# Delta heads: value projected first and turned by VectorE and permuting loads, instead of by TensorE chunk by chunk

## The chip, the cores and the metric

The kernel runs on one core of one Trainium2 chip. The metric is the device time of one execution in microseconds (us); the figure for a kernel is the median of its runs. A core has TensorE (PE: matmuls, and PEld: loads of the stationary operand), VectorE (DVE), ScalarE (ACT), GpSimd (POOL) and SyncE (SP), each with its own queue of instructions in order; SP, ACT and POOL issue the DMAs here.

## The reference

A hybrid residual block on 1024 tokens of width 1024: a gated linear attention branch of 4 heads, a gated delta branch of 8 heads of width 128, a gated merge of both, then an MLP with squared ReLU. What matters here is one delta head:

```python
d_qkv = jax.nn.silu(causal_short_conv(d_qkv, gdn_conv_w))     # 4 taps
q, k = l2_norm(q), l2_norm(k)
# per chunk, with the triangular solve giving u and w
v_new = uu - w @ state
o     = (q * exp(gc)) @ state + att @ v_new
state = dec * state + k_state.T @ v_new
...
o_d = rms_norm(o_d, gdn_onorm_w) * silu(d_g)
```

## The kernel before, in words

All products are in float32 split into a high and a low part, three passes each. Every projection of the delta branch is one call of `dense_b`: 8 steps (`dense_k`) of 6 matmuls 128x512, into one of two PSUM tiles `pm` with channels on the partitions and 1024 tokens along the row. A delta head is `gdn_head(h)`, which calls `dense_b` three times: 24 steps. After each step `tick()` advances a clock, and `on(t, fn)` puts work of the head into an agenda that runs it t steps after the head's begin. So the order on each engine is the order of this agenda, between the steps of the dense product; a number above 24 means that the work runs under the next head's projections. The names in the trace: `pm<-hH,wH`, `pm<-hL,wH`, `pm<-hH,wL` are the three passes of a dense step; `cv` is a projection after its convolution, `si` its tanh, and a product of the two makes silu; `pa` is any of four small PSUM banks.

The projections come in the order q, value, gate. `conv_silu` takes the three taps, the tanh and the silu of one; q's run at ticks 9 to 14, the value's at 18 to 22. `att` (two halves) makes q times k per chunk on TensorE at ticks 15 and 16, VectorE multiplies by the decays `Dt`. `squares` (`qj`) and `qd` (q times the decay, in `eg`) are at 15. `ktok` (`kt`), k with tokens on the partitions, comes from DRAM through four permuting loads of POOL, each of 32 partitions in pieces of 32 floats.

The state goes through 8 chunks of 128 tokens, each in three ticks. `c0(t)`, tick 24 + 3t: TensorE turns the value's chunk (a matmul with `ident`) into a fresh bank and adds `ke` times the state `st` to it, ScalarE scales it to `rs`. `c1(t)`, a tick later: the inverse `U` times `rs`, which ScalarE copies twice, scaled (`vs`) and plain (`vn`; both are halves of one tile, named `vn` in the trace). `c2(t)`: `kt` times `vs` gives the state's update, which VectorE adds (`st`), and two products give the output in `po`. The outputs of heads 0 to 4 then go through a norm whose factors are laid out by two DMAs (`on_d`, `row`). `u1`, `u2`, `u3` complete the head's inverse at ticks 7, 10 and 13. During head 7 the merging stage starts, with branch weights `wB` (POOL and SP) and stored outputs `xq` (SP).

The weights of projections come in the order of a table, `plan`, whose last entry tells which engine makes the low part.

Of the kernel before, what the change touches and what calls it, by code (L numbers as in the profile page):

```python
# [8 lines left out]
F32 = mybir.dt.float32  # L9
# [3 lines left out]
AF = mybir.ActivationFunctionType  # L13
ALU = mybir.AluOpType
# [5 lines left out]
NT = 8  # L20
EPS = 1e-6
C_AQ, C_AK, C_AV, C_AG, C_LR = 0, 512, 1024, 2048, 3072
C_DQ, C_DK, C_DV, C_DG, C_BETA, C_DA, C_MA, C_MD = 3088, 4112, 5136, 6160, 7184, 7192, 7200, 8224
# [27 lines left out]
def block_kernel(ctx: ExitStack, tc: tile.TileContext, x, c, ada_w, ada_b, pre_mix_w, post_mix_w,  # L51
# [3 lines left out]
    x, ada_w, w_in, gla_w_lr = x[0], ada_w[0], w_in[0], gla_w_lr[0]  # L55
# [4 lines left out]
    sm = ctx.enter_context(tc.tile_pool(name="sm", bufs=3))  # L60
# [4 lines left out]
    dr = ctx.enter_context(tc.tile_pool(name="dr", bufs=1, space=DRAM))  # L65

    V, A, G, T = engines = [InOrder(tc, e) for e in (nc.vector, nc.scalar, nc.gpsimd, nc.tensor)]
# [3 lines left out]
    def nm(p):  # L71
        uid[0] += 1
        return f"{p}{uid[0]}"
# [3 lines left out]
    def t4(shape=(128, 1024), dt=F32, p="t", tag="w4"):  # L77
        return w4.tile(list(shape), dt, tag=tag, name=nm(p), bufs=tag_bufs[tag])
# [4 lines left out]
    def pat(shape=(128, 512)):  # L83
        return pa.tile(list(shape), F32, tag="pa", name=nm("pa"))
# [58 lines left out]
    vt = t4((95, 128), p="vt")  # L143
# [277 lines left out]
    for hh in range(4):  # L421
        plan += [(w_in, C_AQ + hh * 128, 128, 8, V), (w_in, C_AK + hh * 128, 128, 8, V),
                 (w_in, C_AV + hh * 256, 256, 4, V), (w_in, C_AG + hh * 256, 256, 8, V)]
    plan += [(w_in, c0 + h * 128, 128, 8, E) for h in range(8) for c0, E in ((C_DQ, (1, 5) if h else (4, 6)), (C_DV, (1, 3)), (C_DG, (1, 4)))]

    def conv_w_later(raw_ap, shape, dh, dl, src=None):

# [18 lines left out]
    def splits():  # L446
        early = {}

        def load(e):
            early[e] = load_raw(*plan[e][:3])  # L450

        first = next(e for e, p_ in enumerate(plan) if p_[1] == C_DQ)
        for e, (w, c0, n, kt, E) in enumerate(plan):
            raw = early.pop(e) if e > first else load_raw(w, c0, n)
            if e < 3:
                for i in range(2):
                    part = raw[:, :, i * 128:(i + 1) * 128]
                    yield conv_w_later(part, (128, 8, 128), *E) if e or i else conv_w_tile(part, (128, 8, 128), E=V)
            elif type(E) is tuple:
                if e + 1 < len(plan):  # L460
                    at(E[1] + 1, lambda: load(e + 1))
                yield conv_w_later(raw, (128, 8, 128), *E)
            elif kt == 4:
                yield [conv_w_tile(raw[:, 4 * i:4 * i + 4, :], (128, 4, 256), E=E) for i in range(2)]
            else:
                for i in range(n // 128):
                    yield conv_w_tile(raw[:, :, i * 128:(i + 1) * 128], (128, 8, 128), E=E)
        yield None
# [8 lines left out]
    def dense_b(rhs):  # L477
        wH, wL = next_w()
        ps = pmt()
        for k in range(8):  # L480
            dense_k(ps, wH, wL, rhs, k)
            tick()
        return ps
# [425 lines left out]
    oa_d = [dr.tile([2, 128, 1024], F32, name=f"oa_d{i}") for i in range(4)]  # L909
    od_d = [dr.tile([2, 128, 1024], F32, name=f"od_d{i}") for i in range(4)]  # L910
    on_d = [dr.tile([1024], F32, name=f"on_d{h}") for h in range(8)]
    kg_d = [dr.tile([128, 1024], F32, name=f"kg_d{h}") for h in range(4)]

    def gdn_head(h, then=None):
# [3 lines left out]
        def on(t, fn):  # L918
            at(begin + t - clock[0], fn)
# [38 lines left out]
        def conv_silu(ps, ct, t, late=0):  # L958

            y, u = t4(p="cv"), {}  # L960
            A.activation(y, ps, AF.Copy, scale=ccol[:, 3 * 24 + ct:3 * 24 + ct + 1])

            def tap(s_):
                V.scalar_tensor_tensor(y[:, s_:], ps[:, :S - s_], ccol[:, (3 - s_) * 24 + ct:(3 - s_) * 24 + ct + 1],
                                       y[:, s_:], ALU.mult, ALU.add)

            def tanh():
                u["t"] = t4(p="si")
                A.activation(u["t"], y, AF.Tanh)

            t += late
            for s_ in (1, 2, 3):
                on(t + s_, lambda s_=s_: tap(s_))
            on(t + 4, tanh)
            on(t + 6 - late, lambda: V.scalar_tensor_tensor(y, u["t"], 1.0, y, ALU.add, ALU.mult))
            return y

        on(7, u1)
        on(10, u2)
        on(13, u3)  # L980
        psq = dense_b(h_rhs)

        q = conv_silu(psq, h, 8)
        z, turned = {}, h < 5
        vq = None if turned else small(8, "vq")

        def att(hf):
            if not hf:
                z["att"] = t4(p="attT")
            pt = pat()  # L990
            for i in range(4):
                sl = slice((hf * 4 + i) * 128, (hf * 4 + i + 1) * 128)
                T.matmul(pt[:, i * 128:(i + 1) * 128], kT[:, sl], q[:, sl], start=True, stop=True)
            on(16 + hf, lambda: V.tensor_mul(z["att"][:, hf * 512:(hf + 1) * 512], pt, Dt[:, hf * 512:(hf + 1) * 512]))

        def squares():
            z["qj"] = t4(p="qj")
# [29 lines left out]
        qd = eg  # L1027
        on(13, lambda: A.activation(eg, eg, AF.Exp))
        on(13, lambda: V.tensor_tensor(ke, kT, ke, ALU.mult))
        on(15, lambda: att(0))  # L1030
        on(16, lambda: att(1))
        on(15, squares)
        on(15, lambda: V.tensor_tensor(qd, q, eg, ALU.mult))
        on(28, lambda: token_part(0))
        on(30, lambda: token_part(1))
        if not turned:
            on(32, token_total)
        psv = dense_b(h_rhs)

        vv = conv_silu(psv, 16 + h, 16, 1)  # L1040
        so = small(32, "so", 1) if turned else small(8, "so", 2)
        c = {"st": None}

        def c0(t):

            sl = slice(t * 128, (t + 1) * 128)
            pv = c["pv"] = pat()
            T.matmul(pv[:, 0:128], vv[:, sl], ident, start=True, stop=(t == 0), is_transpose=True)
            if t:
                T.matmul(pv[:, 0:128], ke[:, sl], c["st"], start=False, stop=True)  # L1050
            rs = c["rs"] = sm.tile([128, 128], F32, tag="rs", name=nm("rs"), bufs=2)
            A.activation(rs, pv[:, 0:128], AF.Copy, scale=rbC[:, h * 8 + t:h * 8 + t + 1])

        def c1(t):

            pv = c["pv"][:, 128:256]
            T.matmul(pv, U[:, t, :], c["rs"], start=True, stop=True)
            v2 = c["vn"] = sm.tile([128, 256], F32, tag="gst", name=nm("vn"), bufs=3)
            if t < NT - 1:
                A.activation(v2[:, 0:128], pv, AF.Copy, scale=ksC[:, h * 8 + t:h * 8 + t + 1])  # L1060
            A.copy(v2[:, 128:256], pv)

        def c2(t):
            sl = slice(t * 128, (t + 1) * 128)
            i, hf, st, vs, vn = t % 4, t // 4, c["st"], c["vn"][:, 0:128], c["vn"][:, 128:256]
            if t < NT - 1:
                pS = c["pv"][:, 256:384]
                T.matmul(pS, ktok[:, sl], vs, start=True, stop=True)
                sn = c["st"] = sm.tile([128, 128], F32, tag="st", name=nm("st"), bufs=3)
                if t:  # L1070
                    V.scalar_tensor_tensor(sn, st, decB[:, h * 8 + t:h * 8 + t + 1], pS, ALU.mult, ALU.add)
                else:
                    A.copy(sn, pS)
            if i == 0:
                c["po"] = pat()
            po = c["po"]
            for j, (l, r) in enumerate(((vn, z["att"][:, sl]), (st, qd[:, sl]))[:1 + min(t, 1)]):
                l, r = (l, r) if turned else (r, l)
                T.matmul(po[:, i * 128:(i + 1) * 128], l, r, start=j == 0, stop=j == min(t, 1))
            if i == 3:  # L1080
                on(47 + late if hf else 35, lambda: (outs if turned else results)(hf, po))
# [42 lines left out]
        def sums(hf):  # L1124
            if not hf:
                c["t"] = t4(p="sqt")
            h_ = slice(hf * 512, (hf + 1) * 512)
            V.transpose(c["t"][:, h_], c["sq"][:, h_])
            V.reduce_sum(so[:, hf * 16:(hf + 1) * 16], r3(c["t"][:, h_], 16), axis=mybir.AxisListType.X)
# [22 lines left out]

        def times():
            V.tensor_mul(sg, sg, c["row"])
            on(75, lambda: A.dma_start(od_d[h // 2][h % 2], sg))
            dump("odT", sg, lambda t: t[h * 128:(h + 1) * 128, :])

        def last_on(t, fn):
# [7 lines left out]
            then()  # L1166
        if turned:
            for t, fn in ((48, lambda: half_squares(0)), (50, lambda: half_squares(1)), (53, lambda: sums(0)),
                          (56, lambda: sums(1)), (58, gated), (59, groups), (62, roots), (66, rows), (72, times)):
                last_on(t, fn)  # L1170
        else:
            on(48 + end, norm)
            on(50 + end, scale)
            on(52 + f_, lambda: fin(0))
            on(53 + f_, lambda: fin(1))
# [1382 lines left out]
```

## Time and profile before

| | |
|---|---|
| median of 3 runs | 1872.37 us (1872.29 to 1873.21) |
| profiled execution | 1873.31 us, its span 1871.6 us |
| TensorE busy | 1845.7 us, 99% |
| VectorE busy | 1415.8 us, 76% |
| ScalarE busy | 864.2 us, 46% |
| GpSimd busy | 204.4 us, 11% |
| mean granted clock of TensorE | 0.998 |
| DMA | 318.00 MB, mean 170 GB/s |

The delta heads run from about 560 to 960 us of the span. All work is recorded with the line of one helper, line 38, so groups are told apart by their tiles. A row of a timeline gives start, duration, engine, operation, output from inputs, and in brackets how long the engine sat idle before it and for whom; PEld idle before a load is not always idle time of PE.

### The profile page before, as it was taken

Reading aid. Unit: us, or ns where it says so; the run is one execution under the profiler, and the core shown is the slowest. Engines: PE = TensorE matmul, PEld = TensorE weight load, DVE = VectorE, ACT = ScalarE, POOL = GpSimd, SP = SyncE. Lnnn points to the kernel's source line nnn. Section 1 sums busy time; section 2 is a strip of 40 time slices with the busy share of each in tenths; the row PEclk is TensorE's granted clock in tenths of the full one; section 3 lists DMA queues with packets and bytes.
Section 4 is the critical chain, followed back from the end, with each engine's and each line's share of the span. In section 5 each row is a group of like instructions: output and inputs, shape, how many; then the busy total and the mean of one; then the engine's idle time right before and its main releaser. Section 6 shows DMA issues by size and latency. Waiting matters only on the chain. (4 is left out here: it accounts for less than half of the span.)

```text
span 1871.6 us, 26161 instructions
## 1 busy us (share of the span) xinstructions
PE 1845.7 (99%) x10025; PEld 1547.4 (83%) x10025; DVE 1415.8 (76%) x2205; ACT 864.2 (46%) x1389; POOL 204.4 (11%) x196
## 2 busy tenths in 40 slices
PE   7999999999999999999999999999999999999998
PEld 5788888989888888888888888878888888888886
DVE  5785844968766677778788688986687877778887
ACT  5454324243333444444654555568545446343333
POOL 2120111111120011111101001000022210000001
PEclk9999999999999999999999999999999999999999
DMA  9686573324235454555868757346667668163425
GB/s 317 219 259 192 154 170 102 107 74 136 68 103 173 112 145 134 157 146 174 242 180 205 231 142 195 90 172 210 206 220 252 210 236 308 57 226 112 157 102 102
DMA packets 255070, 318.00 MB, mean 170 GB/s; under 512 B 73474, under 2 KB 179408, under 8 KB 254944
## 3 DMA queue, kind: packets, MB, share of 16 engines
q1 hardware_dynamic: 222032, 272.63, 45.3%
q0 software_dynamic: 16640, 28.73, 7.9%
q10 hardware_dynamic: 16272, 14.95, 2.5%
q8 instruction: 79, 1.29, 0.3%
q14 instruction: 47, 0.39, 0.1%
HBM read 233.77 MB, written 82.51 MB: 169 GB/s over the span
## 5 line engine op out<-in xcount | busy, mean ns | idle before, releaser
L38 PE MATMUL pm<-hH,wH 128*128 128x512 f32 x864 | 284.7, 410 | 0.0
L38 PE MATMUL pm<-hL,wH 128*128 128x512 f32 x864 | 269.3, 392 | 0.0
L38 PE MATMUL pm<-hH,wL 128*128 128x512 f32 x864 | 267.5, 390 | 0.0
L38 PE MATMUL pm<-oH,wB 128*128 128x512 f32 x672 | 214.8, 394 | 0.6 <-DMA wB<-in_w_branch_gla_dram 0.6
L38 PE MATMUL pa<-w,yH 128*128 128x512 f32 (+1 forms) x696 | 212.5, 387 | 0.0
L38 PEld LDWEIGHTS pm<-hH,wL 128*128 128x128 f32 x864 | 161.7, 188 | 35.5
L38 PEld LDWEIGHTS pm<-hL,wH 128*128 128x128 f32 x864 | 161.9, 188 | 34.9
L38 PEld LDWEIGHTS pm<-hH,wH 128*128 128x128 f32 x864 | 147.1, 190 | 19.2 <-issue 0.2
L38 DVE TENSOR_TENSOR w<-raw,w 128x512 fp32r<-128x512 f32 (+1 forms) x144 | 125.8, 876 | 40.9 <-ACT w L38 40.0
L38 PEld LDWEIGHTS pa<-w,yH 128*128 128x128 f32 x696 | 130.1, 188 | 27.0 <-DVE ya L38 0.4
L38 PEld LDWEIGHTS pm<-oH,wB 128*128 128x128 f32 x672 | 126.1, 188 | 26.8 <-DMA wB<-in_w_branch_gla_dram 1.1
L38 ACT CAST w<-raw 128x512 fp32r<-128x512 f32 (+1 forms) x144 | 99.5, 711 | 89.3 <-DVE raw L38 80.0
L38 PE MATMUL pa<-w,yL 128*128 128x512 f32 (+1 forms) x348 | 134.5, 387 | 0.0
L38 PE MATMUL pm<-oL,wB 128*128 128x512 f32 x336 | 130.8, 389 | 0.0
L38 ACT CAST wH<-raw 128x1024 fp32r<-128x1024 f32 x62 | 64.4, 1046 | 112.8 <-PE pm L38 72.1
L38 PE MATMUL pa<-oB,w 128*128 128x512 f32 x480 | 111.9, 391 | 0.8 <-DVE oB L38 0.5
L38 PEld LDWEIGHTS pa<-oB,w 128*128 128x128 f32 x480 | 89.6, 188 | 20.2 <-DVE oB L38 1.2
L38 DVE TENSOR_TENSOR wL<-raw,wH 128x1024 fp32r<-128x1024 f32 x62 | 75.4, 1219 | 38.2 <-ACT wH L38 37.6
L38 DVE SCALAR_TENSOR_TENSOR cv<-pm,ccol,cv 128x1023 f32<-128x1023 f32 (+2 forms) x72 | 91.9, 1276 | 8.5 <-ACT cv L38 7.4
L38 PE MATMUL pa<-oT,w 128*128 128x512 f32 x384 | 90.8, 389 | 0.0
L38 PE MATMUL pm<-oT,w 128*128 128x512 f32 x384 | 90.8, 389 | 0.0
L38 DVE TENSOR_TENSOR ya<-pa,ya 128x512 f32<-128x512 f32 (+1 forms) x83 | 56.0, 682 | 43.7 <-PE pa L38 43.7
(427 smaller groups left out, 3750.0 us busy)
## 6 DMA issues: line engine op xcount, KB each, us to landing
yL<-y_d SPq DMA_DIRECT2D x53, 512.0 KB, 7.4
raw<-in_mlp_w_dram SPq DMA_DIRECT2D x23, 1024.0 KB, 6.1
raw<-in_w_in_dram SPq DMA_DIRECT2D x18, 1024.0 KB, 7.3
raw<-in_w_in_dram SPq DMA_DIRECT2D x32, 512.0 KB, 4.9
araw<-in_ada_w_dram SPq DMA_DIRECT2D x32, 512.0 KB, 3.8
raw<-in_mlp_w_dram SPq DMA_DIRECT2D x18, 512.0 KB, 4.9
araw<-in_ada_w_dram SPq DMA_DIRECT2D x32, 256.0 KB, 6.6
sl<-sg_d SPq DMA_DIRECT2D x16, 512.0 KB, 7.3
```

The costliest lines, as they stand in the source:

```text
L38: r = fn(*args, **kw)
```

## The change

Delta heads project value, q, gate. The value's conv and silu come first (silu now a tick earlier, at 13). `v_turn` transposes it in 32x32 blocks on VectorE (two instructions of 128x512, tick 14), SP stores it to a new DRAM tile `v_d` (tick 15), and POOL loads it back in four pieces that permute the blocks, as `kt` does, into `vt` with tokens on the partitions (tick 17). `att`, `squares` and `qd` move from ticks 15 and 16 to 23 and 24. In the chunks, `c0` has no transpose: for the first chunk `rs` is made from `vt` in SBUF; for later ones the state product is accumulated on the value that `c1` of the chunk before has copied (ScalarE, `vt` to PSUM) over the place from which `vs` and `vn` were read. The `kt` product in that bank no longer starts its group anew. The last product of the norm and its store move by one tick.

On TensorE, the first and second ticks of a chunk (second chunk of head 1), before:

```order
L38 MATMUL pm_6018<-hH_562,wL_5971 128x512 x2
L38 MATMUL pa_6050<-ident,cv_5905 128x128
L38 MATMUL pa_6050<-st_6038,ke_5760 128x128
L38 MATMUL pm_6018<-hH_564,wH_5921 128x512 x2
L38 MATMUL pm_6018<-hL_579,wH_5921 128x512 x2
L38 MATMUL pm_6018<-hH_564,wL_5971 128x512 x2
L38 MATMUL pa_6050<-rs_6053,U_5337 128x128
```

and after, in the same place:

```order
L38 MATMUL pm_6040<-hH_570,wL_5980 128x512 x2
L38 MATMUL pa_6047<-st_6063,ke_5777 128x128
L38 MATMUL pm_6040<-hH_572,wH_5931 128x512 x2
L38 MATMUL pm_6040<-hL_587,wH_5931 128x512 x2
L38 MATMUL pm_6040<-hH_572,wL_5980 128x512 x2
L38 MATMUL pa_6093<-rs_6075,U_5345 128x128
```

The product with `ident` is gone; the state product goes into the bank of the chunk before, and the product with `U` takes a new one.

On ScalarE, in the same chunk of head 1, before:

```order
L38 ACTIVATE rs_6053<-pa_6050,rbC 128x128
L38 ACTIVATE vn_6071<-pa_6050,ksC 128x128
L38 COPY vn_6071<-pa_6050 128x128
L38 ACTIVATE rs_6102<-pa_6099,rbC 128x128
L38 ACTIVATE vn_6111<-pa_6099,ksC 128x128
```

and after:

```order
L38 ACTIVATE rs_6075<-pa_6047,rbC 128x128
L38 ACTIVATE vn_6095<-pa_6093,ksC 128x128
L38 COPY vn_6095<-pa_6093 128x128
L38 COPY pa_6093<-vt_5926 128x128
L38 ACTIVATE rs_6124<-pa_6093,rbC 128x128
L38 ACTIVATE vn_6135<-pa_6133,ksC 128x128
```

A copy from `vt` follows `vn`, into the bank from which the next `rs` is made and into which the product with `kt` goes next; that product waits for ScalarE, now for this copy.

On POOL, at the loads of head 2, before:

```order
L38 DMA on_d_485<-sqt_6088 32x32
L38 DMA kt_6537<-kt_d_451 32x32x32
L38 DMA row_6335<-on_d_485 128x1024
L38 DMA kt_6537<-kt_d_451 32x32x32 x3
L38 DMA on_d_486<-sqt_6492 32x32
```

and after:

```order
L38 DMA on_d_485<-sqt_6113 32x32
L38 DMA vt_6334<-v_d_495 32x32x32 x4
L38 DMA row_6351<-on_d_485 128x1024
L38 DMA kt_6570<-kt_d_451 32x32x32 x4
L38 DMA on_d_486<-sqt_6525 32x32
```

The four loads of `vt` stand between the store of the norm's factors and the load of their row; the next head's `kt` follows. In head 7 the loads of `vt` stand behind one load of branch weights `wB`.

The diff, without the table's line (it exchanges q and value in `plan` and keeps the engines by place) and the two lines of `times` (72 to 73, 75 to 76):

```diff
+    v_d = [dr.tile([128, 1024], F32, name=f"v_d{h}") for h in range(8)]
...
-            on(t + 6 - late, lambda: V.scalar_tensor_tensor(y, u["t"], 1.0, y, ALU.add, ALU.mult))
+            on(t + 5 - late, lambda: V.scalar_tensor_tensor(y, u["t"], 1.0, y, ALU.add, ALU.mult))
...
-        psq = dense_b(h_rhs)
-
-        q = conv_silu(psq, h, 8)
+        psv = dense_b(h_rhs)
+        vv = conv_silu(psv, 16 + h, 8)
...
-            on(16 + hf, lambda: V.tensor_mul(z["att"][:, hf * 512:(hf + 1) * 512], pt, Dt[:, hf * 512:(hf + 1) * 512]))
+            on(24 + hf, lambda: V.tensor_mul(z["att"][:, hf * 512:(hf + 1) * 512], pt, Dt[:, hf * 512:(hf + 1) * 512]))
...
-        on(15, lambda: att(0))
-        on(16, lambda: att(1))
-        on(15, squares)
-        on(15, lambda: V.tensor_tensor(qd, q, eg, ALU.mult))
+
+        def v_turn():
+            z["vb"] = t4(p="vb")
+            for h_ in (slice(0, 512), slice(512, 1024)):
+                V.transpose(z["vb"][:, h_], vv[:, h_])
+
+        def v_load():
+            z["vt"] = t4(p="vt")
+            src = v_d[h].rearrange("(c i) (t b j) -> b i t c j", i=32, t=8, j=32)
+            for b_ in range(4):
+                G.dma_start(z["vt"][32 * b_:32 * b_ + 32].rearrange("i (t c j) -> i t c j", t=8, j=32), src[b_])
+
+        on(14, v_turn)
+        on(15, lambda: DMA.dma_start(v_d[h], z["vb"]))
+        on(17, v_load)
+        on(23, lambda: att(0))
+        on(24, lambda: att(1))
+        on(23, squares)
+        on(23, lambda: V.tensor_tensor(qd, q, eg, ALU.mult))
...
-        psv = dense_b(h_rhs)
-
-        vv = conv_silu(psv, 16 + h, 16, 1)
+        psq = dense_b(h_rhs)
+        q = conv_silu(psq, h, 16, 1)
...
-            pv = c["pv"] = pat()
-            T.matmul(pv[:, 0:128], vv[:, sl], ident, start=True, stop=(t == 0), is_transpose=True)
+            rs = c["rs"] = sm.tile([128, 128], F32, tag="rs", name=nm("rs"), bufs=2)
+            src = z["vt"][:, sl]
             if t:
-                T.matmul(pv[:, 0:128], ke[:, sl], c["st"], start=False, stop=True)
-            rs = c["rs"] = sm.tile([128, 128], F32, tag="rs", name=nm("rs"), bufs=2)
-            A.activation(rs, pv[:, 0:128], AF.Copy, scale=rbC[:, h * 8 + t:h * 8 + t + 1])
+                src = c["pv"][:, 128:256]
+                T.matmul(src, ke[:, sl], c["st"], start=False, stop=True, skip_group_check=True)
+            A.activation(rs, src, AF.Copy, scale=rbC[:, h * 8 + t:h * 8 + t + 1])
...
-            pv = c["pv"][:, 128:256]
+            bank = c["pv"] = pat()
+            pv = bank[:, 128:256]
...
             A.copy(v2[:, 128:256], pv)
+            if t < NT - 1:
+                A.copy(pv, z["vt"][:, (t + 1) * 128:(t + 2) * 128])
...
-                T.matmul(pS, ktok[:, sl], vs, start=True, stop=True)
+                T.matmul(pS, ktok[:, sl], vs, start=False, stop=True, skip_group_check=True)
```

More of the change, by code (lines that the diff above doesn't have):

```diff
@@ L423, in block_kernel @@
                  (w_in, C_AV + hh * 256, 256, 4, V), (w_in, C_AG + hh * 256, 256, 8, V)]
-    plan += [(w_in, c0 + h * 128, 128, 8, E) for h in range(8) for c0, E in ((C_DQ, (1, 5) if h else (4, 6)), (C_DV, (1, 3)), (C_DG, (1, 4)))]
+    plan += [(w_in, c0 + h * 128, 128, 8, E) for h in range(8) for c0, E in ((C_DV, (1, 5) if h else (4, 6)), (C_DQ, (1, 3)), (C_DG, (1, 4)))]
     def conv_w_later(raw_ap, shape, dh, dl, src=None):
@@ L450, in load @@
             early[e] = load_raw(*plan[e][:3])
-        first = next(e for e, p_ in enumerate(plan) if p_[1] == C_DQ)
+        first = next(e for e, p_ in enumerate(plan) if p_[1] == C_DV)
         for e, (w, c0, n, kt, E) in enumerate(plan):
@@ L1154, in times @@
             V.tensor_mul(sg, sg, c["row"])
-            on(75, lambda: A.dma_start(od_d[h // 2][h % 2], sg))
+            on(76, lambda: A.dma_start(od_d[h // 2][h % 2], sg))
             dump("odT", sg, lambda t: t[h * 128:(h + 1) * 128, :])
@@ L1168, in gdn_head @@
             for t, fn in ((48, lambda: half_squares(0)), (50, lambda: half_squares(1)), (53, lambda: sums(0)),
-                          (56, lambda: sums(1)), (58, gated), (59, groups), (62, roots), (66, rows), (72, times)):
+                          (56, lambda: sums(1)), (58, gated), (59, groups), (62, roots), (66, rows), (73, times)):
                 last_on(t, fn)
```

## The prediction

> **What bounds the kernel now.** I read the busy shares first, then the windows of the delta stage, then who waits for whom there.
>
> ```profile
> span 1871.6 us, 26161 instructions
> PE 1845.7 (99%) x10025; PEld 1547.4 (83%) x10025; DVE 1415.8 (76%) x2205; ACT 864.2 (46%) x1389; POOL 204.4 (11%) x196
> ```
>
> The windows' first and last of that stage (PE, PEld, DVE, ACT, POOL busy, then clock, DMA share, GB/s):
>
> ```profile
> 585.00:635.00 50.00, 50.00 (x293) 42.22 (x292) 30.86 (x41) 17.62 (x35) 4.64 (x6) 1.00 0.39 114
> 885.00:935.00 50.00, 49.45 (x296) 41.58 (x295) 36.94 (x47) 32.18 (x68) 7.77 (x6) 1.00 0.88 254
> ```
>
> TensorE is busy for 50.00 of 50 us early and 49.45 late, at clock 1.00. Time is won by taking work off TensorE and lost by making it wait; work elsewhere is free until TensorE waits for it. The waits from 570 to 1000 us (total us, times, longest):
>
> ```profile
> ACT rs L38 <- PE pa L38: 107.6, 60, 5.6
> ...
> ACT si L38 <- PE pa L38: 9.4, 5, 1.9
> ...
> PEld pa L38 <- ACT vn L38: 2.9, 8, 0.5
> ...
> PEld pa L38 <- DVE st L38: 1.4, 2, 0.9
> ```
>
> ScalarE waits for TensorE all the time; the other way, the weight queue waits for `vn` only 8 times and for the state twice.
>
> **Transposes removed.** One per chunk and head:
>
> ```profile
> L38 PE MATMUL pa<-ident,cv x64: 270/272/274, 593.8 to 958.2; 128*128 128x128 f32 x64
> ```
>
> By durations that is 64 x 0.272 = 17.4 us. But durations of a pipelined engine overlap, so I take distances between starts, each over four matmuls of the dense product and whatever stands between them:
>
> ```profile
> 567.78 0.62 PE L38 MATMUL pm<-hH,wL 128*128 128x512 f32 x2
> ...
> 568.68 0.39 PE L38 MATMUL pm<-hL,wH 128*128 128x512 f32 x1
> ...
> 593.30 0.62 PE L38 MATMUL pm<-hH,wL 128*128 128x512 f32 x2
> ...
> 594.33 0.63 PE L38 MATMUL pm<-hL,wH 128*128 128x512 f32 x2
> 594.79 0.62 PE L38 MATMUL pm<-hH,wL 128*128 128x512 f32 x2
> ...
> 595.93 0.63 PE L38 MATMUL pm<-hL,wH 128*128 128x512 f32 x2
> ...
> 598.23 0.62 PE L38 MATMUL pm<-hH,wL 128*128 128x512 f32 x2
> 598.69 0.27 PE L38 MATMUL pa<-ident,cv 128*128 128x128 f32 x1
> ...
> 599.48 0.39 PE L38 MATMUL pm<-hL,wH 128*128 128x512 f32 x1
> ```
>
> With nothing between, 0.90; with a transpose alone (the first chunk of a head, 593.30), 1.03; with the one product of the next step (594.79), 1.14; with transpose and state product (598.23), 1.25. So a transpose costs 0.13 alone and 1.25 - 1.14 = 0.11 beside a product. Saved: 8 x 0.13 + 56 x 0.11 = **7.2 us**; 17.4 would be the upper end.
>
> The Trainium skill ("TensorE: Matmul & The Clock Gate", Part 4: PE-mode transpose) gives about 275 ns for a 128x128 transpose inside a kernel. The row's 272 ns agrees as a duration; were it the cost of the slot, the sum would gain 17.6 us. The four distances speak against that.
>
> **The copy added.** After `vs` and `vn` of a chunk ScalarE copies the next chunk's value into PSUM, 7 x 8 = 56 times; by the order below, the product with `kt` now waits for it. No copy from SBUF to PSUM is in this trace. Nearest: copies and what uses them.
>
> ```profile
> 595.93 0.26 ACT L38 COPY vn<-pa 128x128 f32<-128x128 f32 x1
> 596.08 1.06 ACT L38 CAST wH<-raw 128x1024 fp32r<-128x1024 f32 x1
> ...
> 684.58 0.59 ACT L38 COPY ob<-pa 128x512 f32<-128x512 f32 x1 [1.57 <-PE pa L38]
> ...
> 686.40 0.62 ACT L38 ACTIVATE sqo<-ob 128x512 f32<-128x512 f32 x1
> ```
>
> ```profile
> 596.63 0.42 PEld L38 LDWEIGHTS pa<-vn,kt 128*128 128x128 f32 x2
> ```
>
> A 128x128 copy takes 0.26; a source in SBUF (sqo, 0.62) costs 0.03 more than one in PSUM (ob, 0.59). At best the copy starts 0.15 after `vn` does, as the cast at 596.08, and ends 0.15 after `vn`'s end at 596.19. But it overwrites what `vn` reads, so I take the other end: it starts when `vn` ends and takes 0.30, to 596.49. The weight load stands at 596.63 without having waited. The copy therefore fits with 0.14 to spare, and costs nothing in an ordinary step; the cover is gone once it takes over about 0.4. As ScalarE's time, 56 x 0.30 = 17 us lie in an engine busy 17.6 to 32.2 of 50.
>
> It costs where the load already waits for `vn`:
>
> ```profile
> 664.34 1.06 ACT L38 ACTIVATE si<-cv 128x1024 f32<-128x1024 f32 x1 [1.87 <-PE pa L38]
> ...
> 665.55 0.25 ACT L38 COPY vn<-pa 128x128 f32<-128x128 f32 x1
> ```
>
> ```profile
> 665.86 0.30 PEld L38 LDWEIGHTS pa<-vn,kt 128*128 128x128 f32 x2 [0.49 <-ACT vn L38]
> ...
> 911.57 0.30 PEld L38 LDWEIGHTS pa<-vn,kt 128*128 128x128 f32 x2 [0.20 <-ACT vn L38]
> ...
> 921.90 0.31 PEld L38 LDWEIGHTS pa<-vn,kt 128*128 128x128 f32 x2 [0.15 <-ACT vn L38]
> ```
>
> At 665.86 the tanh held ScalarE (itself waiting for TensorE, 5 such waits in all, in five heads), and the load began 0.06 after `vn` ended. Each of the 8 waits grows by the copy: 8 x 0.30 = **+2.4 us** (1.2 if it overlaps `vn`). Behind the waiting load stand the output products and the next dense step, so this is TensorE's own time.
>
> **Moved work.** The attention products, `qj` and `qd` go from ticks 15 and 16 to 23 and 24: the same count, so nothing for TensorE as long as q is ready; its silu ends near tick 22, and one tick (two passes of 0.90 hold four of six matmuls) is over 1.35 us. In head 7, tick 23 meets the merging stage:
>
> ```profile
> 929.69 0.34 DVE L38 SCALAR_TENSOR_TENSOR st<-st,decB,pa 128x128 f32<-128x128 f32 x1
> ```
>
> ```profile
> 930.09 0.30 PEld L38 LDWEIGHTS pa<-st,ke 128*128 128x128 f32 x2 [0.91 <-DVE st L38]
> ```
>
> There the load already waits 0.91 for the state. The moved `qd` (about 1.21, the size of the row at 666.82 below) and two attention halves now come just ahead on VectorE, and `qj` ahead of `vn` on ScalarE. Between 0 and their 2.6 us, I take **+1.2**, the one full-size multiply.
>
> **The value's new way.** v is turned on VectorE, stored by SP (512 KB), loaded by POOL in four permuting pieces. VectorE's 16 halves of 0.70 are 11 us of an engine that is busy 31 to 37 of 50.
>
> ```profile
> 666.82 1.21 DVE L38 SCALAR_TENSOR_TENSOR cv<-si,cv 128x1024 f32<-128x1024 f32 x1
> ...
> 927.22 0.70 DVE L38 STREAM_TRANSPOSE sqt<-qj 128x512 f32<-128x512 f32 x1
> ```
>
> ```profile
> kt_d<-ktok SPq DMA_DIRECT2D x8, 512.0 KB, 2.8
> kt<-kt_d POOLq DMA_DIRECT2D x32, 128.0 KB, 6.0
> ```
>
> ```profile
> 633.05 3.91 POOL L38 DMA_DIRECT2D kt<-kt_d  x4 [45.36 <-PE pa L38]
> ...
> 903.28 1.35 POOL L38 DMA_DIRECT2D wB<-in_w_branch_gla_dram  x1 [31.38 <-DVE attT L38]
> ```
>
> ```profile
> 686.13 0.37 ACT L38 ACTIVATE rs<-pa,rbC 128x128 f32<-128x128 f32 x1 [0.96 <-PE pa L38]
> ```
>
> In head 2 the silu of the first projection stands at 666.82 now and comes a tick earlier; with `ke`, the state and two halves of 0.70 around it, v is turned by about 669.5. The store lands 2.8 later, 672.3; the last of four loads is issued 2.9 after (3/4 of 3.91) and lands 6.0 on, 681.2. The first `rs` runs at 686.13: spare 4.9 us, less what VectorE, SP and POOL hold it up. I cost it at 0. The state update of that step comes behind the silu, 1.21 later, in five heads; its product is in the next tick's slot, so I bound this by 0 and 0.2 each and take 0. The row load and the next `kt`, behind these loads on POOL, come 3.9 later at most, each far ahead of its use. In head 7 a branch weight load goes out on POOL ahead of `vt` (1.35), and the DMA is at 0.88 of its time, against 0.39 early; twice the landing time leaves 4.9 - 1.4 - 6.0 = -2.5. So 0 to 2.5 once; I take 0.
>
> The Trainium skill ("DMA: Bandwidth & Descriptors", Specifications) wants at least 512 bytes per transfer for full rate; these pieces are 128 bytes. The `kt` row has that form and lands in 6.0 us, which is in the sum already; were the rule to cost more under load, that is the late-value rival below, which no row here settles.
>
> **Sum.** -7.2 + 2.4 + 1.2 = **-3.6 us**. The profiled execution took 1873.31 (span 1871.6 and 1.7 around it), 0.94 above the median; it would go to 1869.7, and the median from 1872.37 to **1868.8**.
>
> **Rivals.** *Full gain* (0.17): the copy overlaps `vn` and the moved work finds room; -7.2 + 1.2 = -6.0, or 1866.4. For: ScalarE's next instruction does start under `vn`. Against: same PSUM region.
>
> *Ordinary steps wait* (0.17): the copy takes longer than 0.4, and the 48 other steps wait too. At 0.1 each that is +4.8, net +1.2 or 1873.6; at 0.15, +7.2, net 3.6 or 1876.0. It turns into a loss at 3.6/48 = 0.075 each, a copy of about 0.46. Against: nothing of that size takes more than 0.37 here.
>
> *Value late* (0.16), on the slower side: `vt` lands after the first `rs` needs it, in all heads. It decides from 3.6/8 = 0.45 us a head, about 5.4 later than reckoned; 1 us a head gives 8 - 3.6 = +4.4, 1876.8. For: four engines or queues in a row, DMA at 0.88 in head 7. Against: 4.9 us of room.
>
> *Transposes by their duration* (0.02): -17.4 + 3.6 = -13.8, 1858.6.
>
> **Chances.** The forecast's own case (0.48) reaches from -1.5 to -5.5. A measurement here tells about 0.2% from no change, 3.7 us, and the forecast lies on that line: half of it counts as faster. Faster: 0.24 + 0.17 + 0.02 = 0.43. Slower: half of the two bad rivals, 0.17. Same: the rest, 0.40. The range, 1865 to 1876, takes in full gain and the milder half of the bad cases; the likeliest case alone is 1866.9 to 1870.9.
>
> **What would show it.** No `ident,cv` on TensorE; starts in a chunk's first slot 1.14 apart, not 1.25; copies into PSUM of 0.30; the load after them waiting about 0.8 at the five tanh places and nowhere in ordinary steps; first `rs` of each head waiting for no DMA. Weight loads waiting for the copy in most chunks, or for `vt`, would make this wrong.

## The result and the profile after

The changed kernel took 1882.91 us (median of 4 runs, 1881.52 to 1884.42) against 1872.72 before (4 runs, 1872.29 to 1873.21): a ratio of 1.0055 (95% interval 1.0037 to 1.0072), 10 us slower. The forecast was 1868.8, with a range of 1865 to 1876.

The page after, busy shares:

```profile
span 1882.2 us, 26120 instructions
PE 1842.8 (98%) x9961; PEld 1543.4 (82%) x9961; DVE 1425.4 (76%) x2221; ACT 878.6 (47%) x1445; POOL 234.4 (12%) x228
```

TensorE is busy 2.9 us less and the span is 10.6 us longer, so it sits idle 39.4 us instead of 25.9. The windows (PE, PEld, DVE, ACT, POOL busy, clock, DMA share, GB/s) tell where. Two of them before:

```profile
735.00:785.00 50.00, 49.33 (x292) 41.19 (x291) 38.27 (x69) 21.88 (x45) 5.04 (x6) 1.00 0.55 150
...
935.00:985.00 50.00, 49.38 (x251) 40.93 (x250) 43.77 (x65) 27.47 (x53) 2.56 (x2) 1.00 0.64 184
```

And after:

```profile
685.00:735.00 50.00, 48.11 (x280) 40.10 (x280) 36.70 (x61) 23.31 (x52) 11.29 (x14) 1.00 0.58 174
735.00:785.00 50.00, 46.63 (x271) 38.55 (x270) 38.76 (x69) 21.93 (x49) 8.62 (x11) 1.00 0.50 155
785.00:835.00 50.00, 48.17 (x280) 40.10 (x279) 37.73 (x62) 23.07 (x50) 10.69 (x12) 1.00 0.58 168
835.00:885.00 50.00, 47.13 (x278) 39.30 (x277) 40.13 (x79) 22.95 (x63) 8.94 (x10) 1.00 0.51 147
...
935.00:985.00 50.00, 45.36 (x217) 37.63 (x217) 36.88 (x60) 28.57 (x68) 3.85 (x3) 0.93 0.61 172
```

TensorE is idle for 1.8 to 3.4 us in each of the four windows of the middle heads, against at most 0.7 before, and for 4.6 us in the last, where the clock falls too. The waits from 570 to 1000 us (total us, times, longest) name the releaser:

```profile
PEld pa L38 <- DVE st L38: 16.6, 11, 5.0
DVE sqt L38 <- DMA od_d<-si: 13.5, 4, 3.8
...
DVE raw L38 <- DMA wq<-in_w_branch_gla_dram: 5.8, 1, 5.8
PEld pa L38 <- ACT pa L38: 4.5, 7, 0.7
...
PEld pa L38 <- DVE sqr L38: 2.4, 1, 2.4
...
ACT rs L38 <- DMA vt<-v_d: 1.1, 2, 0.6
```

Before, the second of these rows read:

```profile
DVE sqt L38 <- DMA od_d<-si: 0.5, 1, 0.5
```

The state product waits 11 times for VectorE, and VectorE itself waits for two DMAs that the prediction does not mention: the store of the head's output (`od_d`) and the branch weights `wq`. The seven waits for the copy come to 4.5 us, where the same loads waited 2.9 us for `vn` before; the value's load costs ScalarE 1.1 us. The first loss, in rows of ScalarE, VectorE and the weight queue at head 3:

```profile
691.15 0.33 ACTq L38 DMA_DIRECT2D od_d<-si  x1
```

```profile
692.15 0.35 DVE L38 SCALAR_TENSOR_TENSOR st<-st,decB,pa 128x128 f32<-128x128 f32 x1
695.81 0.71 DVE L38 STREAM_TRANSPOSE sqt<-sqo 128x512 f32<-128x512 f32 x1 [3.32 <-DMA od_d<-si]
...
700.30 0.35 DVE L38 SCALAR_TENSOR_TENSOR st<-st,decB,pa 128x128 f32<-128x128 f32 x1
```

```profile
700.70 0.30 PEld L38 LDWEIGHTS pa<-st,ke 128*128 128x128 f32 x2 [1.90 <-DVE st L38]
```

The store goes out at 691.15 and lands about 4.6 later. VectorE, whose next instruction writes `sqt` into the buffer that this store still reads, stands still for 3.32 us; the state update behind it on VectorE comes late, and TensorE waits 1.90. The store was moved by one tick, about 1.9 us (a head of 24 ticks takes some 46); it also lands later after its issue there, 5.1 us (median) against 4.0 before. The second loss, in head 7:

```profile
944.77 1.23 DVE L38 TENSOR_TENSOR raw<-wq,raw 128x1024 f32<-128x1024 f32 x1 [5.84 <-DMA wq<-in_w_branch_gla_dram]
```

```profile
950.55 0.50 PEld L38 LDWEIGHTS pa<-st,ke 128*128 128x128 f32 x2 [5.04 <-DVE st L38]
```

```profile
945.00:950.00 5.00, 0.95 (x5) 0.42 (x3) 4.93 (x8) 1.04 (x1) 0.00 (x0) 0.88 0.73 116
950.00:955.00 5.00, 4.45 (x13) 3.67 (x14) 4.93 (x6) 3.54 (x14) 0.00 (x0) 0.50 0.00 0
955.00:960.00 5.00, 5.00 (x27) 4.25 (x26) 3.49 (x5) 0.57 (x2) 0.00 (x0) 0.94 0.00 0
```

VectorE waits 5.84 us for weights of the merging stage, with the state update behind it. TensorE's weight queue waits 5.04, and the granted clock falls while it waits (it is 0.50 from 949 to 950). The low clock costs time only while TensorE works: half of the 4.45 us that it is busy in the second window and 0.06 of the third, about 2.5 us more.

### The profile page after: what moved, and what is told of

Same layout as the page of the kernel before. It is cut to its first block, busy times and chain, and to the rows that moved or that the text cites. A ratio compares the mean times of both kernels' runs of the same rounds, so it can differ in the third digit from the quotient of the medians.

```text
span 1882.2 us, 26120 instructions
## 1 busy us (share of the span) xinstructions
PE 1842.8 (98%) x9961; PEld 1543.4 (82%) x9961; DVE 1425.4 (76%) x2221; ACT 878.6 (47%) x1445; POOL 234.4 (12%) x228
```

## The experiments

All are timed against the kernel before on the same chip (1872.38 to 1872.65 there); the differences between two experiments are partly across chips, so a few tenths of a us in them mean nothing.

**One thing undone: the store back a tick earlier** (`e1_store_earlier`).

```diff
-... (66, rows), (73, times)):
+... (66, rows), (72, times)):
-            on(76, lambda: A.dma_start(od_d[h // 2][h % 2], sg))
+            on(75, lambda: A.dma_start(od_d[h // 2][h % 2], sg))
```

> The changed kernel with one thing undone: the last product of the norm and the store of the head's output are back at ticks 72 and 75 (they had moved to 73 and 76). Theory S (the store came a tick later; the buffer it frees is the one that VectorE's sqt takes, so VectorE stands still and with it the state update): the waits of sqt for od_d fall from 13.5 us to under 3, the state product's waits at about 700.7, 748.1, 756.0 and 798.0 (1.9, 1.7, 1.9, 1.8) go, minus 5 to 7 us: 1876 to 1878. Rival V (VectorE is simply behind because of the work moved onto it, and the wait for the store only shows it): sqt waits less but the state is as late, within 2 us of 1882.9.

Measured: 1873.57 us, 1.0009 of before (1.0000 to 1.0018), 9.3 less than the changed kernel. VectorE's wait for the store and the state's:

```profile
PEld pa L38 <- DVE st L38: 8.2, 8, 4.3
...
DVE sqt L38 <- DMA od_d<-si: 1.5, 4, 0.5
```

The gain is larger than the 5 to 7 that I expected. Besides the direct waits (1.9, 1.7 and 1.8) the ones that follow shrink (from 1.94 to 0.79 at 755.97, from 0.57 to 0.20 at 713.81), where VectorE had not yet caught up. I had also overlooked the fourth head: there it is not the state but `sqr`, the sums of q's squares, that comes late, and the 2.40 us that TensorE waited for it at 844.01 are gone too. At the old ticks VectorE waits for no `row` either, so moving this product had gained nothing.

**The same thing alone, on the kernel before** (`e3_before_store_later`: 72 to 73 and 75 to 76, nothing else).

> The kernel before with the one thing done alone: the last product of the norm at tick 73 and the store at 76 instead of 72 and 75. Theory S: sqt's waits for od_d rise from 0.5 us (1 time) to about 2 us in each of four heads, the state product waits 0.5 to 1.5 us in three or four of them: plus 1 to 4 us, 1874 to 1877. Rival V: no change, 1872 to 1873.5.

Measured: 1881.25 us, 1.0047 (1.0032 to 1.0062): 8.9 us slower. VectorE's and the weight queue's rows at the place shown above:

```profile
696.75 0.71 DVE L38 STREAM_TRANSPOSE sqt<-sqo 128x512 f32<-128x512 f32 x1 [3.36 <-DMA od_d<-si]
```

```profile
701.63 0.30 PEld L38 LDWEIGHTS pa<-st,ke 128*128 128x128 f32 x2 [1.66 <-DVE st L38]
```

The same wait (3.36 for 3.32) without a single moved projection, turn or copy. So the work added to VectorE is ruled out as the cause of this wait. My size of 1 to 4 was too low: `sqt` waits 13.4 us in all, as in the changed kernel, and TensorE has five waits of 1.65 to 1.80 us behind it, 8.5 us in all, where the kernel before had one of 0.51. Product and store moved together in both runs; that it is the store is what the rows of `sqt` name.

**Head 7 turned on TensorE** (`e2_head7_transposed`).

```diff
+        by_dma = h < 7
+        if by_dma:
             on(14, v_turn)
             on(15, lambda: DMA.dma_start(v_d[h], z["vb"]))
             on(17, v_load)
...
+            if not by_dma:
+                c["pv"] = pat()
+                src = c["pv"][:, 0:128]
+                T.matmul(src, vv[:, sl], ident, start=True, stop=(t == 0), is_transpose=True)
+                if t:
+                    T.matmul(src, ke[:, sl], c["st"], start=False, stop=True)
```

> The changed kernel, but head 7 alone turns its value on TensorE as before (no v_d store, no vt loads, no copies in that head; order of projections as changed). Theory D (in head 7 the turned value's store and small-piece loads meet a full DMA, the branch weights come later, VectorE waits 5.8 us for wq and TensorE 5.0 for the state, and its clock drops): the 5.0 us wait and the slow clock go, minus 6 to 9 us with 1 us of transposes coming back: 1874 to 1877. Rival M (the merging stage is late because att, qd and qj were moved into it): the wait for wq stays at 4 us or more, within 2 us of 1882.9.

Measured: 1877.18 us, 1.0027 (1.0017 to 1.0037), 5.7 less than the changed kernel, a little under the 6 to 9 expected. The state's longest wait is 1.9 instead of 5.0, and TensorE is busy 49.98 of the 50 us from 935 on, at a clock of 1.00.

**The kernel before without 56 transposes** (`e4_no_transposes`).

```diff
-            T.matmul(pv[:, 0:128], vv[:, sl], ident, start=True, stop=(t == 0), is_transpose=True)
             if t:
-                T.matmul(pv[:, 0:128], ke[:, sl], c["st"], start=False, stop=True)
+                T.matmul(pv[:, 0:128], ke[:, sl], c["st"], start=True, stop=True)
+            else:
+                T.matmul(pv[:, 0:128], vv[:, sl], ident, start=True, stop=True, is_transpose=True)
```

> The kernel before, leaving out the transpose of the value in chunks 2 to 8 of each head (56 transposes; those chunks are computed from the state product alone), nothing added. By the distances of starts (0.11 each) minus 6.2 us: 1866. By the instructions' durations (0.272 each) minus 15.2: 1857. If the transposes lie in gaps that exist anyway: no change.

Measured: 1867.61 us, 0.9975 (0.9965 to 0.9985): 4.8 less by medians, 0.085 per transpose (0.05 to 0.12 by the interval). The profile counts TensorE's busy time:

```profile
span 1865.2 us, 26018 instructions
PE 1839.4 (99%) x9969; PEld 1544.4 (83%) x9969; DVE 1415.9 (76%) x2205; ACT 864.7 (46%) x1389; POOL 203.4 (11%) x196
```

TensorE is busy 6.3 us less than before, 0.113 per transpose; its duration of 0.272 is no measure of its price. Both counts are far from the 15.2 us of the durations.

**Both repairs together** (`e5_both`).

> The changed kernel with both repairs: last product of the norm and store back at 72 and 75, and head 7's value turned on TensorE. If the two losses are separate they add: 1882.9 - 9.3 - 5.7 = 1867.9, 1867 to 1869, with no wait of TensorE over 1 us before 920 but the tanh places. If both are one loss (lateness that the first hands to head 7), the second repair adds little: 1872 to 1873.5.

Measured: 1868.49 us, 0.9977 (0.9967 to 0.9986). The two losses add: 9.3 + 5.7 = 15.0 expected, 14.4 found.

**`ke` a little later**, on top of that (`e6_ke_later`).

```diff
-        on(13, lambda: V.tensor_tensor(ke, kT, ke, ALU.mult))
+        on(16, lambda: V.tensor_tensor(ke, kT, ke, ALU.mult))
```

> As e5_both, and the multiply of ke on VectorE at tick 16 instead of 13. The state update of tick 13 then stands behind the silu alone, as far back as it stood behind ke before the change. Expected if the silu and ke together make the state late: the state product's waits of 0.2 us in each of heads 2 to 6 go, 1 us less than e5_both. Rival: another piece of VectorE's work takes the gap; no change.

Measured: 1867.45 us, 0.9970 (0.9959 to 0.9981), 1.0 less. With both repairs the state product behind the silu and `ke` waits in five heads, 0.20 or 0.21 us in four and 0.80 in one; none of these waits is left, though another grows (from 0.79 to 1.10 at 752.79). The time agrees, though the intervals overlap.

**The copy behind the `kt` product**, on top of that (`e7_copy_after_kt`).

```diff
             A.copy(v2[:, 128:256], pv)
-            if t < NT - 1 and by_dma:
-                A.copy(pv, z["vt"][:, (t + 1) * 128:(t + 2) * 128])
...
+            if t < NT - 1 and by_dma:
+                A.copy(c["pv"][:, 128:256], z["vt"][:, (t + 1) * 128:(t + 2) * 128])
             if i == 0:
                 c["po"] = pat()
```

> As e6_ke_later, and ScalarE's copy of the next value into PSUM comes after the product with kt and the state update, not before. If that product's waits for the copy are what the copy costs, the waits at the five tanh places fall from about 0.72 to 0.49 idle of the weight queue and the ones in head 7 do not exist: 1.2 to 1.5 us less than e6_ke_later. Rival: the next state product, which now waits for update and then copy, becomes late: the same time or slower.

Measured: 1866.03 us, 0.9965 (0.9951 to 0.9979), 1.4 less, again with intervals that overlap. A tanh place with the copy ahead of the product (as in e6) and behind it (this kernel), weight queue:

```profile
710.94 0.30 PEld L38 LDWEIGHTS pa<-vn,kt 128*128 128x128 f32 x2 [0.71 <-ACT pa L38]
```

```profile
708.48 0.30 PEld L38 LDWEIGHTS pa<-vn,kt 128*128 128x128 f32 x2 [0.41 <-ACT vn L38]
```

The wait is for `vn` again and 0.30 shorter, at all five places: 1.5 us. The rival's wait, of the next state product for the copy, appears once (1.32 us at 750.55, where e6 waited 1.10 for the state). This version has the lowest median of all that ran, 6.6 us below the kernel before.

**What in head 7 costs.** Three kernels like the one with both repairs, whose head 7 also does part of the value's way, unused: all of it (`e8_head7_loads_unused`, the diff below); the turn and the store alone, without its last line (`e9_head7_store_only`); or, in `e10_head7_one_load`, turn, store and one contiguous load, `G.dma_start(t4(p="vt"), v_d[h])`, in place of that line.

```diff
+        else:
+            on(14, v_turn)
+            on(15, lambda: DMA.dma_start(v_d[h], z["vb"]))
+            on(17, v_load)
```

> As e5_both, but head 7 also turns its value on VectorE, stores it and loads it in the four permuting pieces, without using it (TensorE turns it as before). Theory D (the store and the loads themselves, on POOL and in a full DMA, delay the branch weights): VectorE waits 4 us or more for wq and TensorE as long for the state; 4 to 6 us more than e5_both. Rival C (head 7's copies and its use of the loaded value): as fast as e5_both, within 1.5 us.

> As e5_both, but head 7 also turns its value on VectorE and stores it, unused; no loads. The extra of e8_head7_loads_unused over e5_both was 4.6 us. Theory Q (the store waits for the turned value at the head of SP's queue and holds the xq loads behind it by 5 us): the xq loads start as late as with the loads, most of the 4.6 is there: 1872 to 1873.5. Theory L (POOL's four loads in small pieces): within 1 us of e5_both, 1868 to 1869.5. Theory T (bytes moved, half of them here): 1870 to 1871.5.

> As e9_head7_store_only, and the stored value is loaded back by POOL in one contiguous load instead of four permuting ones, unused. Theory Q: as e9, 1872 to 1873.5. Theory L: the small pieces are gone, as e5_both, 1868 to 1869.5. Theory T: as e8_head7_loads_unused, 1872.5 to 1873.5, while e9 is between.

Measured: 1873.05 us with all of it (1.0002, 0.9993 to 1.0011), 1870.09 with the store (0.9987, 0.9977 to 0.9996), 1870.19 with the one load (0.9987, 0.9977 to 0.9997). Against 1868.49 the turn and store cost 1.6, the contiguous load 0.1, and doing it in four permuting pieces 2.9. So 4.6 us come although nobody uses the value (theory C falls), and none of my three theories has it alone. POOL's queue with both repairs, and with all of the loads:

```profile
898.28 1.35 POOL L38 DMA_DIRECT2D wB<-in_w_branch_gla_dram  x1 [22.36 <-ACT wB L38]
...
919.40 1.27 POOL L38 DMA_DIRECT2D wq<-in_w_branch_gla_dram  x1 [6.91 <-DMA wq<-in_w_branch_gla_dram]
```

```profile
897.51 1.35 POOL L38 DMA_DIRECT2D wB<-in_w_branch_gla_dram  x1 [22.36 <-ACT wB L38]
899.20 3.97 POOL L38 DMA_DIRECT2D vt<-v_d  x4 [0.34 <-issue]
...
924.66 2.62 POOL L38 DMA_DIRECT2D wq<-in_w_branch_gla_dram  x2 [12.94 <-DMA wq<-in_w_branch_gla_dram]
```

POOL's `wq`, which adds onto what SP has loaded, goes out at 924.66 instead of 919.40. POOL was free; it waited 12.94 us for the half of `wq` that SP loads first. SP's rows (a row merges several issues), with both repairs and with all of the loads:

```profile
893.90 11.96 SPq L38 DMA_DIRECT2D xq<-oa_d  x6
906.86 1.06 SPq L38 DMA_DIRECT2D wq<-in_w_branch_gla_dram  x2
```

```profile
895.73 0.32 SPq L38 DMA_DIRECT2D v_d<-vb  x1
...
898.87 7.57 SPq L38 DMA_DIRECT2D xq<-oa_d  x6
906.54 6.61 SPq L38 DMA_DIRECT2D wq<-in_w_branch_gla_dram  x2
```

Behind the store only the first of the six `xq` loads is issued 5 us later (898.87 for 893.90); taken one by one, the other five go out from 899 to 906 in both kernels, and the first `wq` at 906.86 and 906.54. So the half that POOL waits for is not issued late. It lands late: 12.0 us after its issue with both repairs and 17.4 with all of the loads, 14.7 with the store alone and 15.0 with the one load:

```profile
wq<-in_w_branch_gla_dram SPq DMA_DIRECT2D x1, 512.0 KB, 12.0
```

```profile
wq<-in_w_branch_gla_dram SPq DMA_DIRECT2D x1, 512.0 KB, 17.4
```

`xq` lands after 11.7 us (median) instead of 7.0, and after 9.3 with the one load. That speaks for the DMA's load, at a share of 0.94 to 0.98 in these kernels, and against theory Q's blocked queue.

The step from 1.7 to 4.6 us has the clock in it as well. TensorE waits 3.53 us for the state with all of the loads, and then works at half the clock:

```profile
940.00:945.00 5.00, 5.00 (x14) 4.03 (x14) 3.99 (x4) 2.49 (x13) 0.00 (x0) 0.50 0.00 0
```

That is 14 matmuls in 5 us where both repairs have 29, or 2.5 us lost in this window. With the store alone and with the one load the longest wait for the state is 1.6 us, and the clock stays at 1.00. So most of the 2.9 us is by these rows not the price of the four loads as such, but of a wait long enough for the clock to fall; no run separates the two. Nor was it separated how much of the later landing is POOL's four issues and how much the 128-byte pieces.

## Why the prediction was wrong

**Where it failed.** Its sum has no term for `times`, the last product of the norm, and its store, which move by one tick. The prediction asked of the moved work only whether TensorE's own input is ready, and named `att`, `qj` and `qd`; that the store frees the buffer in which VectorE's `sqt` is written, one or two ticks later, was not looked at, though the kernel before had VectorE wait for it (at most 0.5 us) already. It is worth 9.3 us undone, 8.9 us done alone, where the sum had nothing.

The second failure is the step on head 7's loads: "0 to 2.5 once; I take 0". I priced the lateness of `vt` itself, not what its transfers do to the others in a full DMA: `wq` lands late, and with it `raw` and the state update on VectorE. `vt` itself landed 10.6 us after its issue in head 7, near the doubled 6.0 of the forecast, and was only 0.56 us late there, on ScalarE alone. The others cost 5.7 us net of the eight transposes that the test took back, about 2.5 of it by the clock, for which the sum had no term either. Both failures are of one kind: I followed what the change adds, and not what it makes late beside it.

**What held.** The transposes: 0.11 each forecast, 0.113 measured in busy time and 0.085 in device time. The Trainium skill ("TensorE: Matmul & The Clock Gate", Part 4: PE-mode transpose) gives about 275 ns for a transpose inside a kernel, which again fits the duration; as an estimate from that figure 56 of them would come to 15.4 us, and taking them out made TensorE 6.3 us less busy. The copy: 0.27 measured for 0.30,

```profile
L38 ACT COPY pa<-vt x56: 269/270/271, 595.5 to 966.1; 128x128 f32<-128x128 f32 x56
```

ordinary steps do not wait for it, and the five tanh places wait 0.71 instead of the forecast 0.8. What it costs at these places was 1.4 us (e7 against e6); the 2.4 forecast had 1.5 for them and 0.9 for head 7, which has no copies in e6. One bound of the rival on ordinary steps was added up wrong: with 0.14 to spare the loss begins at a copy of about 0.52, not 0.46; at 0.27 nothing hung on it. The value's way: the first `rs` waits for `vt` twice, 1.1 us, on ScalarE alone, so the late-value rival did not come about.

**What was smaller or larger.** The silu ahead of the state: bounded by 0.2 a head and taken as 0, it was that upper end together with `ke`, 1.0 us (e6). The moved work in head 7: +1.2 forecast; at its place the state product waits 1.06 in the changed kernel (934.62) and 1.50 with both repairs (925.73), as against 0.91 before, so it was 0.2 to 0.6.

**The sum without the two.** With both repairs the kernel is 4.2 us faster than before on that chip; the sum was -3.6, and the repaired kernel has the eight transposes of head 7 back (+1.0) and lacks that head's copies. The terms that I had add up to within about a microsecond, which is in part luck: the silu was 1.0 too low, and the moved work 0.6 to 1.0 too high. The two losses that I had at nothing were four times as large as the forecast gain.

None of the rivals was the case that happened. The slower one, the late value, had a late DMA in view, but one that holds TensorE through ScalarE; the real ones held it through VectorE.

## What to carry to other kernels

A step that moves by one tick moves the moment when its buffer comes free: for every store that a change delays, look for the next writer of that buffer, and for what stands behind that writer on its engine. A transfer added to a full DMA must be priced by what it makes late, not by whether it arrives; with the DMA at 0.94 to 0.98 of its time that price was 4.6 us for 1 MB, and its turn on VectorE, that nobody used, in good part through the clock. And the cost of a short matmul among long ones is read from distances between starts: 0.11 us against a duration of 0.27.

## What the runs showed of the hardware

A long wait of TensorE costs more than its length. In head 7 the granted clock fell to 0.50 during waits of 5.04 us (the changed kernel), 4.31 (the store back) and 3.53 (all of the loads, unused), and it was still 0.50 in the first 5 to 6 us of work after them, which cost 2.5 to 3 us on top. The waits of 1.90 and 2.40 us in the middle heads left it at 1.00; where between 2.40 and 3.53 it begins to fall, no run here shows.

A 512 KB load of branch weights landed 12.0 us after its issue with the DMA at a share of 0.94 (885 to 935 us), 14.7 with a store of 512 KB more, 15.0 with that store and one contiguous load of 512 KB, and 17.4 when that load came in four permuting pieces of 128 KB, with the share at 0.98 in all three.
